# A hybrid trunk on one core: a second convolution chunk on VectorE, its taps spread among the S5 states, and TensorE's small products of the even mixer in blocks

## The chip, the cores and the metric

The kernel runs on one core of a Trainium2 chip. The core has five engines with instruction streams of their own: TensorE (PE in the profile; PEld are its weight loads), VectorE (DVE), ScalarE (ACT), GpSimd (POOL) and SyncE (SP), which here only issues transfers. Engines wait for each other by semaphores, and each works through its instructions in the order in which they were put on it. What counts is the device time of one execution in microseconds. The kernel before has a median of 1348.53 us over three runs (1348.24 to 1348.56).

## What is computed

One sequence of 512 positions with 1024 channels goes through two layers, each a mixer and a gated feed-forward block, with a norm ahead of each, residual adds, and a final norm. All values are float32. The even layer's mixer joins four retention heads with a Mamba-2 state-space part of 16 heads in chunks of 128 positions; the odd layer's joins a causal depthwise convolution over 31 positions with an S5 state-space part:

```python
def even_mixer(h, ...):
    ...
    r = head_group_norm(retention_chunkwise(q, k, v)).reshape(b, l, RET_V)
    y_ret = jax.nn.silu(g) * r
    ...
    y = ssd_chunked(xs, dt, a_neg, bm, cm)      # y_diag + y_off
    ...
def ssd_chunked(...):
    ...
    y_diag = jnp.einsum("bcijgh,bcjghp->bcighp", cb[..., None] * lmat, X)
    y_off = jnp.einsum("bcign,bcghpn->bcighp", Cc, prev) * jnp.exp(acs)[..., None]

def odd_mixer(h, ...):
    ca, cg, u = split_cols(h @ w_in, [512, 512, 512])
    c = ca * jax.nn.sigmoid(cg)
    c = causal_dwconv(c, conf_dw_w, conf_dw_b)                 # 31 taps, per channel
    c = jax.nn.silu(layer_norm(c, conf_ln_g, conf_ln_b))
    s = jax.nn.gelu(s5_ssm(u, ...))
    s = s * jax.nn.sigmoid(s @ s5_glu_w)
    return jnp.concatenate([c, s], axis=-1) @ w_out
```

## The kernel before

**Layout and stages.** Channels lie on the 128 partitions and the 512 positions along a row, so a tensor of 512 channels is four tiles of 128 x 512. The stages follow each other: even mixer, feed-forward, odd mixer, feed-forward, final norm. A projection (`proj`) splits weights and inputs into a high and a low part in a reduced float format and makes three matmuls for each 128 channels (`mm3`, L100 to L102). `wload` fetches the weights on SyncE's queue into `wraw` (four buffers), ScalarE casts the high part `whi` (L90), and VectorE subtracts to get the low part `wlo` (L91). `split` (L95, L96) does the same to inputs: `sh` on ScalarE and `slo` on VectorE for the S5 result, for instance. Matmuls that write `pyo`, `pyd`, `pcv`, `pS`, `pY` and the transposes are not of the split kind; they read float32 as it is.

**What sets the order.** The program is written in a certain order, and a scheduler with its own estimates of time lays the instructions out on each engine; `issue_after(x)` forbids it to put what follows ahead of `x`. Tiles come from rotating pools, so a load can wait until a buffer is free.

**Even mixer, `pair`.** Each of eight pairs of heads builds `ar` (decays times products, two tiles), `X` and the states `prev`. Then `pyo` gets three matmuls of 128 x 128 (L453; chunks 1 to 3, each from `prev` of the chunk before), and `pyd` eight of 64 x 128 (L458; four chunks of two heads). A matmul of this kind shows as two records in the profile. They stand on TensorE among the projections of whatever comes next (`pg`, `pxbc`, `po`), and the scheduler may put projections between them.

**Even mixer, `head`.** The normed result `yn` of each retention head is transposed in eight pieces (`pyT`, L564) to two tiles.

**Odd mixer.** `glu_in(i)` projects `ca` and `cg` of convolution chunk i. For a chunk in the list `PECONV` it writes the product twice to half-shifted tiles `cx` (VectorE, L848; the shifted halves copied by ScalarE, L850), and `conv_pe(i)` runs the 31 taps as 32 matmuls on TensorE (`pcv`, L891, 64 records), with weights `kd` that `conv_loads(i)` fetches in four transfers of 256 KB on SyncE's queue. Chunk 0 is not in the list: `conv(0, ...)` makes 30 multiply-adds on VectorE (L875), each on a whole tile with another shift, on top of a first tap by ScalarE. `s5_in(q)` projects `u`; `s5_state(q)` transposes it on TensorE (`pu2`, `puT`, with ScalarE's copies L916 and L922 between), makes the inputs of the states (`pS`, L930) and runs a chain of small VectorE operations (`s5rot`, L934 to L954) that ends in `sst`. `s5_y(q)` gives `pY` (L971, L974), ScalarE copies it out (L977), and `s5_split(q)` transposes it back (`pyT`, L984), applies the GELU (`sg`, L986) and splits it (`sh`, `slo`). "The S5 residue" in the title of the change is this low part `slo`. All four of them are inputs of the gate projection `pgl`.

The order as written before: chunks and states alternate; chunk 1's convolution stands ahead of `s5_state(3)`, chunk 2's between `s5_y(1)` and `s5_y(2)`, chunk 3's ahead of `s5_split(3)`; and the whole `conv(0)` on VectorE comes last, not before the state 3 chain is done.

**Start and end.** The packed constants `c1` (182 KB) are fetched on ScalarE's queue beside the first input tile, and the eight last output transfers are on SyncE's.

Of the kernel before, what the change touches and what calls it, by code (L numbers as in the profile page):

```python
# [15 lines left out]
P = 128  # L16
T = 512
NT = T // P
# [6 lines left out]
SH = 16  # L25
NPAIR = SH // 2
POOLTAPS = {}
PECONV = (1, 2, 3)
WV0 = (0, 1, 3, 6)
PACK0 = (("g_mix0", KC),)  # L30
PACK1 = (("ident", P), ("tri", P), ("cw", 48), ("cb", 12), ("dtb", SH), ("alog", SH), ("dsk", NPAIR),
         ("snw", NPAIR))
# [4 lines left out]
class Trunk:  # L37
# [197 lines left out]
    def finish(self, st, half, out):  # L235
        nc = self.nc
        ts = slice(half * T // 2, (half + 1) * T // 2)
        last = self.tmp("sq")[:, :T // 2]
        nc.scalar.activation(last, self.x[KC - 1][:, ts], AF.Square)
        self.gain(st, KC - 1, ts)  # L240
        if half == 0:
            st["p"] = self.ps("pstat")
            for t in range(NT):
                nc.tensor.matmul(st["p"][:, t:t + 1], lhsT=st["acc"][:, t * P:(t + 1) * P], rhs=self.onec, start=True,
                                 stop=True)
        p = st["p"][:, 2 * half:]
        for t in range(2):
            mark = nc.tensor.matmul(p[:, NT + t:NT + t + 1], lhsT=last[:, t * P:(t + 1) * P], rhs=self.onec, start=True,
                                    stop=True)
        v = self.small("fin_v", [P, 2])  # L250
        nc.vector.tensor_scalar(v, p[:, :2], 1.0 / D, EPS, op0=ALU.mult, op1=ALU.add)
        nc.vector.scalar_tensor_tensor(v, p[:, NT:NT + 2], 1.0 / D, v, op0=ALU.mult, op1=ALU.add)
        rs = self.rsqrt(v, [P, 2], "fin")
        for t in range(2):
            row = slice((2 * half + t) * P, (2 * half + t + 1) * P)
            for i in range(2):
                p = self.ps("pfin") if i else self.pp("pfin")
                with self.tc.issue_after(mark.ins):
                    for c in range(4):
                        nc.tensor.transpose(p[:, c * P:(c + 1) * P], self.x[4 * i + c][:, row], self.ident)  # L260
                o = self.slot("fin")
                if i == 0:
                    nc.scalar.activation(o, p, AF.Copy, scale=rs[:, t:t + 1])
                else:
                    nc.vector.tensor_scalar(o, p, rs[:, t:t + 1], None, op0=ALU.mult)
                nc.sync.dma_start(out[row, i * T:(i + 1) * T], o)

    def load_params(self):
        self.unpack("c2", PACK2, self.nc.gpsimd)
# [3 lines left out]
    def load_x(self):  # L273
        nc = self.nc
        st = self.norm_begin("mix0")
        st["w"] = []
        for c in range(KC):
            nc.sync.dma_start(self.x[c], self.ins["xT"][c])
            self.norm_chunk(st, c, False)
            if c in WV0:  # L280
                n = min([k for k in (*WV0, KC) if k > c]) - c
                hi, lo = self.wload(self.ins["wv0"][:, c * 272:(c + n) * 272], n * 272)
                st["w"] += [[w[:, k * 272:k * 272 + 272] for w in (hi, lo)] for k in range(n)]
            if c == 0:
                self.unpack("c1", PACK1, nc.scalar)
                self.ident = self.c["ident"]
        return st


    def even(self, st, prep):  # L290
        nc = self.nc
# [114 lines left out]
        def pair(pr, grp):  # L406
# [37 lines left out]
            for c in range(1, NT - 1):  # L444
                for h in range(2):
                    a0, a1 = (c - 1) * P + h * 64, c * P + h * 64
                    nc.vector.scalar_tensor_tensor(pv[:, a1:a1 + 64], pv[:, a0:a0 + 64],
                                                   cdl[:, c, 2 * pr + h:2 * pr + h + 1], p[:, a1:a1 + 64],
                                                   op0=ALU.mult, op1=ALU.add)
            po = self.ps("pyo")  # L450
            for c in range(1, NT):
                s = slice(c * P, (c + 1) * P)
                nc.tensor.matmul(po[:, s], lhsT=pv[:, (c - 1) * P:c * P], rhs=Ct[g][:, s], start=True, stop=True)  # L453
            pd = self.ps("pyd")
            for c in range(NT):
                for h in range(2):
                    s = slice(c * P, (c + 1) * P)
                    nc.tensor.matmul(pd[64 * h:64 * h + 64, s], lhsT=X[:, c * P + 64 * h:c * P + 64 * h + 64],  # L458
                                     rhs=ar[h][:, s], start=True, stop=True)
            y = self.slot("y")  # L460
            nc.vector.scalar_tensor_tensor(y, xc, dsk[:, pr:pr + 1], pd, op0=ALU.mult, op1=ALU.add)
            nc.vector.tensor_tensor(E[:, P:], E[:, P:], po[:, P:], op=ALU.mult)
# [52 lines left out]
        def head(h):  # L515
# [40 lines left out]
            for b in range(NT):  # L556
                s = slice(256 * (b % 2), 256 * (b % 2) + 256)
                nc.scalar.activation(yn[b // 2][:, s], py[b // 2][:, s], AF.Identity, scale=rs[:, b:b + 1],
                                     bias=nm[:, b:b + 1])
            for f in range(2):  # L560
                p = self.ps("pyT")
                for b in range(NT):
                    c0 = 256 * (b % 2) + f * P
                    nc.tensor.transpose(p[:, b * P:(b + 1) * P], yn[b // 2][:, c0:c0 + P], self.ident)  # L564
                nc.vector.tensor_tensor(gs[f], gs[f], p, op=ALU.mult)
                hi, lo = self.slot("mh", F32R), self.slot("ml", F32R)
                self.split(gs[f], hi, lo)
                mix[2 * h + f] = (hi, lo)
# [249 lines left out]
    def odd(self, st):  # L818
# [175 lines left out]
        def s5_loads(q):  # L994
            w1 = [self.slot("w1") for _ in range(2)]
            for ri in range(2):
                ld(w1[ri], self.w1d[ri, q])
            rot = self.slot("rot").rearrange("p (r x) -> p r x", r=2)
            ld(rot, self.rotd[0:2, q // 2, :, 256 * (q % 2):256 * (q % 2) + 256].rearrange("r p x -> p r x"))
            s5w[q] = (w1, rot)  # L1000
            if q % 2 == 0:
                rho = self.slot("rho")
                ld(rho, self.rotd[2, q // 2])
                s5rho[q // 2] = rho
# [13 lines left out]
            sx[q] = (hi, lo)  # L1018

        glu_in(0)  # L1020
        s5_loads(0)
        s5_loads(1)
        s5_in(0)
        glu_in(1)
        s5_state(0)
        s5_in(1)
        s5_loads(2)
        s5_loads(3)
        glu_in(2)
        s5_state(1)  # L1030
        s5_in(2)
        conv_loads(1)
        glu_in(3)
        s5_state(2)
        s5_in(3)
        conv_pe(1)
        states = s5_state(3)
        conv_loads(2)
        for q in range(4):
            out_loads(q)  # L1040
        y2[0] = s5_y(0)
        y2[1] = s5_y(1)
        s5_split(0)
        conv_pe(2)
        conv_loads(3)
        y2[2] = s5_y(2)
        s5_split(1)
        y2[3] = s5_y(3)
        s5_split(2)
        conv_pe(3)  # L1050
        s5_split(3)
        conv(0, after=states)
        mix = [None] * 8
        for m in range(4):
            p = self.pp("pgl")
# [166 lines left out]
```

## Time and profile before

| | us |
|---|---|
| median of three runs | 1348.53 |
| the profiled execution | 1349.29 |
| its span, first to last instruction | 1347.5 |
| one convolution on TensorE, 898.51 to 912.00 in the trace | 13.49 |
| sum of the 30 multiply-adds on VectorE (13.19 + 9.87 busy) | 23.06 |

Prices and places are read in the profiled execution, so sums are made against its 1349.29 us, which is the span and 1.8 us around it. A row of a timeline gives the start, the time from the first start to the last end, the engine, the line, the operation, the output and inputs with their shapes, how many like instructions follow each other, and in brackets the idle time of the engine ahead of it with what ended it. Matmuls overlap, so what one costs is the distance from its start to the next one's start.

### The profile page before, as it was taken

To read this page: it belongs to the slowest core of one execution; us is meant where nothing else is said; L and a number is where in the kernel's file an instruction comes from. 1 tells how busy PE (TensorE), PEld (TensorE's weight loads), DVE (VectorE), ACT (ScalarE), POOL (GpSimd) and SP (SyncE) were. 2 spreads that over 40 slices of the span, in tenths; PEclk is the share of its full clock that TensorE was granted. 3 is DMA by queue.
4 is the path that set the end of the run, shared out by engine and by line. 5 is a ranking of instruction groups with operands and counts; after the bars stand their busy time and mean duration, and the time that the engine had idled before them with its cause. 6 is when DMAs were issued, how large, how long until landed. Compare 5 with 4: busy or idle time off the path is not lost.

```text
span 1347.5 us, 17450 instructions
## 1 busy us (share of the span) xinstructions
PE 1333.4 (99%) x6676; PEld 1088.8 (81%) x6676; DVE 908.1 (67%) x1544; ACT 551.2 (41%) x775; POOL 160.9 (12%) x284
## 2 busy tenths in 40 slices
PE   9999999999999999999999999999999999999997
PEld 8778888888878888888888888557888888888887
DVE  6887877679688889787634346486877777773233
ACT  5454545454334444444423233235644444442221
POOL 0210010000570333860000000000000000000000
PEclk9999999999999999999999999999999999999999
DMA  6532234232264343543333344322433333333321
GB/s 226 158 114 83 71 93 120 70 104 85 79 175 127 116 125 112 151 135 104 90 92 100 98 129 161 125 95 63 134 96 105 97 94 94 96 99 89 100 71 63
DMA packets 50532, 146.16 MB, mean 108 GB/s; under 512 B 6544, under 2 KB 7872, under 8 KB 50448
## 3 DMA queue, kind: packets, MB, share of 16 engines
q1 hardware_dynamic: 44288, 127.49, 30.7%
q0 software_dynamic: 5872, 17.37, 4.5%
q8 instruction: 52, 0.85, 0.3%
q14 instruction: 32, 0.26, 0.1%
q10 hardware_dynamic: 288, 0.19, 0.0%
HBM read 135.03 MB, written 9.99 MB: 108 GB/s over the span
## 4 chain that ended last, share of the span: by engine, by line
PE 94%; DVE 3%; ACT 1%; issue 1%; DMA 0%; SPq 0%; DVEq 0%; ACTq 0%
PE pup L100 12%; PE pup L102 12%; PE pup L101 12%; PE pdn L101 6%; PE pdn L100 6%; PE pdn L102 6%; PE pcv L891 3%; PE po L102 3%; PE po L100 3%; PE po L101 3%; PE pxbc L101 1%; PE pxbc L100 1%; PE pxbc L102 1%; PE pqk L100 1%; PE pg L101 1%; PE pg L100 1%
## 5 line engine op out<-in xcount | busy, mean ns | idle before, releaser
L90 ACT CAST whi<-wraw 128x1024 fp32r<-128x1024 f32 (+3 forms) x246 | 231.2, 940 | 490.3 <-PE pup L101 140.9
L91 DVE TENSOR_TENSOR wlo<-wraw,whi 128x1024 fp32r<-128x1024 f32 (+3 forms) x246 | 269.8, 1098 | 140.7 <-ACT whi L90 140.7
L100 PE MATMUL pup<-xh,whi 128*128 128x512 f32 x704 | 274.7, 390 | 0.0
L102 PE MATMUL pup<-xh,wlo 128*128 128x512 f32 x704 | 274.0, 389 | 0.0
L101 PE MATMUL pup<-xl,whi 128*128 128x512 f32 x704 | 273.9, 389 | 0.0
L102 PEld LDWEIGHTS pup<-xh,wlo 128*128 128x128 f32 x704 | 132.2, 188 | 27.4
L101 PEld LDWEIGHTS pup<-xl,whi 128*128 128x128 f32 x704 | 132.2, 188 | 27.4
L100 PEld LDWEIGHTS pup<-xh,whi 128*128 128x128 f32 x704 | 132.2, 188 | 27.2
L100 PE MATMUL pdn<-acth,whi 128*128 128x512 f32 (+1 forms) x374 | 140.9, 377 | 0.0
L101 PE MATMUL pdn<-actl,whi 128*128 128x512 f32 (+1 forms) x374 | 140.8, 377 | 0.0
L102 PE MATMUL pdn<-acth,wlo 128*128 128x512 f32 (+1 forms) x374 | 140.8, 377 | 0.0
L190 DVE SCALAR_TENSOR_TENSOR ffa<-ffh,c,ffa 128x511 f32<-128x511 f32 (+1 forms) x176 | 134.6, 766 | 3.0
L185 DVE TENSOR_TENSOR ffh<-pup,R 128x512 f32<-128x512 f32 x88 | 60.5, 687 | 65.1 <-PE pup L102 64.9
L232 POOL TENSOR_SCALAR x<-x,c 128x512 f32<-128x512 f32 (+1 forms) x9 | 9.1, 1016 | 734.5 <-ACT acc L128 635.1
L187 ACT ACTIVATE ffa<-ffh,c 128x512 f32<-128x512 f32 x88 | 71.8, 816 | 40.0 <-DVE ffh L185 37.3
L100 PEld LDWEIGHTS pdn<-acth,whi 128*128 128x128 f32 x374 | 70.4, 188 | 13.0
L102 PEld LDWEIGHTS pdn<-acth,wlo 128*128 128x128 f32 x374 | 70.4, 188 | 12.9
L101 PEld LDWEIGHTS pdn<-actl,whi 128*128 128x128 f32 x374 | 70.4, 188 | 12.8
L102 PE MATMUL po<-mh,wlo 128*128 128x512 f32 x192 | 75.7, 394 | 0.6 <-DVE wlo L91 0.6
L100 PE MATMUL po<-mh,whi 128*128 128x512 f32 x192 | 75.4, 394 | 0.7 <-ACT mh L95 0.7
L101 PE MATMUL po<-ml,whi 128*128 128x512 f32 x192 | 75.6, 394 | 0.0
L95 ACT CAST acth<-ffg 128x512 fp32r<-128x512 f32 x44 | 27.3, 621 | 92.8 <-DVE ffg L197 88.2
(418 smaller groups left out, 2220.0 us busy)
## 6 DMA issues: line engine op xcount, KB each, us to landing
wraw<-in_wup_dram SPq DMA_DIRECT2D x88, 512.0 KB, 3.6
wraw<-in_wdn_dram SPq DMA_DIRECT2D x32, 512.0 KB, 3.6
wraw<-in_weo_dram SPq DMA_DIRECT2D x32, 256.0 KB, 3.1
wraw<-in_wxbc_dram SPq DMA_DIRECT2D x12, 512.0 KB, 3.8
wraw<-in_wdn_dram SPq DMA_DIRECT2D x16, 384.0 KB, 3.2
wraw<-in_wz_dram SPq DMA_DIRECT2D x8, 512.0 KB, 3.6
wraw<-in_wg_dram SPq DMA_DIRECT2D x8, 512.0 KB, 3.6
ar<-acd POOLq DMA_DIRECT2D x16, 256.0 KB, 3.8
```

What stands on the lines that cost most here:

```text
L90: nc.scalar.copy(hi[:, :n], raw[:, :n])
L91: (eng or nc.vector).tensor_tensor(lo[:, :n], raw[:, :n], hi[:, :n].bitcast(F32), op=ALU.subtract)
L95: self.nc.scalar.copy(hi, src)
L100: mm(out, lhsT=w[0], rhs=x[0], start=start, stop=False)
L101: mm(out, lhsT=w[0], rhs=x[1], start=False, stop=False)
L102: self.mark = mm(out, lhsT=w[1], rhs=x[0], start=False, stop=stop)
L185: nc.vector.tensor_tensor(h, p, st["R"], op=ALU.mult)
L187: nc.scalar.activation(a, h, AF.Identity, scale=dw[:, j, 2:3], bias=db[:, j:j + 1])
L190: nc.vector.scalar_tensor_tensor(a[:, s:], h[:, :T - s], dw[:, j, tap:tap + 1], a[:, s:], op0=ALU.mult, op1=ALU.add)
L232: self.nc.gpsimd.tensor_scalar(self.x[c][:, ts], self.x[c][:, ts], st["g"][:, c:c + 1], 1.0, op0=ALU.mult, op1=ALU.mult)
L891: self.mark = mm(p[64 * g:64 * g + 64, s:], lhsT=w, rhs=cin[i][g][:, :T - s], start=j == 0, stop=j == 15)
```

## The change

**A.** `PECONV` loses chunk 1, whose 30 taps go to VectorE too. The taps of chunks 0 and 1 are spread over the stage with fixed places: 1 to 8 of chunk 0 behind its product, 9 to 17 not before state 0's chain, 18 to 24 not before state 1's, 25 to 30 and taps 1 to 4 of chunk 1 not before state 2's; 5 to 12 of chunk 1 not before state 3's, and 13 to 30 not before the third `slo`. Chunk 2's convolution on TensorE moves ahead of state 3. **B.** In `pair`, the `pyo` matmuls run in the order 3, 1, 2 in a chain, and `pyd` behind them. **C.** In `head`, the four `pyT` pieces begin with the last, and the others follow it. **D.** `c1` is fetched on SyncE's queue behind the fifth input tile, and one of each two last output transfers goes to ScalarE's queue.

```diff
-PECONV = (1, 2, 3)
+PECONV = (2, 3)
...
-                nc.sync.dma_start(out[row, i * T:(i + 1) * T], o)
+                (nc.sync if i else nc.scalar).dma_start(out[row, i * T:(i + 1) * T], o)
...
-            if c == 0:
-                self.unpack("c1", PACK1, nc.scalar)
+            if c == 4:
+                self.unpack("c1", PACK1, nc.sync)
...
             po = self.ps("pyo")
-            for c in range(1, NT):
-                s = slice(c * P, (c + 1) * P)
-                nc.tensor.matmul(po[:, s], lhsT=pv[:, (c - 1) * P:c * P], rhs=Ct[g][:, s], start=True, stop=True)
+            off = None
+            for c in (3, 1, 2):
+                with self.tc.issue_after(off.ins) if off else nullcontext():
+                    s = slice(c * P, (c + 1) * P)
+                    off = nc.tensor.matmul(po[:, s], lhsT=pv[:, (c - 1) * P:c * P], rhs=Ct[g][:, s], start=True,
+                                           stop=True)
             pd = self.ps("pyd")
-            for c in range(NT):
-                for h in range(2):
+            with self.tc.issue_after(off.ins):
+                for c in range(NT):
+                    for h in range(2):
...
+            first = None
             for f in range(2):
                 p = self.ps("pyT")
-                for b in range(NT):
-                    c0 = 256 * (b % 2) + f * P
-                    nc.tensor.transpose(p[:, b * P:(b + 1) * P], yn[b // 2][:, c0:c0 + P], self.ident)
+                for b in (3, 0, 1, 2):
+                    with self.tc.issue_after(first.ins) if first else nullcontext():
+                        c0 = 256 * (b % 2) + f * P
+                        t = nc.tensor.transpose(p[:, b * P:(b + 1) * P], yn[b // 2][:, c0:c0 + P], self.ident)
+                    first = first or t
...
         glu_in(0)
+        conv(0, range(1, 9))
...
-        s5_state(0)
+        conv(0, range(9, 18), after=s5_state(0))
...
-        s5_state(1)
+        conv(0, range(18, 25), after=s5_state(1))
         s5_in(2)
-        conv_loads(1)
         glu_in(3)
-        s5_state(2)
+        states = s5_state(2)
+        conv(0, range(25, 31), after=states)
+        conv(1, range(1, 5), after=states)
         s5_in(3)
-        conv_pe(1)
+        for i in PECONV:
+            conv_loads(i)
+        conv_pe(2)
         states = s5_state(3)
-        conv_loads(2)
         for q in range(4):
             out_loads(q)
-        y2[0] = s5_y(0)
-        y2[1] = s5_y(1)
-        s5_split(0)
-        conv_pe(2)
-        conv_loads(3)
-        y2[2] = s5_y(2)
-        s5_split(1)
-        y2[3] = s5_y(3)
-        s5_split(2)
+        for q in range(4):
+            y2[q] = s5_y(q)
+            if q:
+                s5_split(q - 1)
         conv_pe(3)
         s5_split(3)
-        conv(0, after=states)
+        conv(1, range(5, 13), after=states)
+        conv(1, range(13, 31), after=ev[2])
```

The first place is TensorE's order at the first pair of the even mixer, before (`pyo` and `pyd` are the pair's two small products, `pg` a retention head's gate projection):

```order
L102 MATMUL pg<-xh,wlo 128x512
L453 MATMUL pyo<-CT,prev 128x128
L458 MATMUL pyd<-ar,X 64x128
L100 MATMUL pg<-xh,whi 128x512
L458 MATMUL pyd<-ar,X 64x128 x4
L453 MATMUL pyo<-CT,prev 128x128
L458 MATMUL pyd<-ar,X 64x128 x2
L453 MATMUL pyo<-CT,prev 128x128
L458 MATMUL pyd<-ar,X 64x128
L101 MATMUL pg<-xl,whi 128x512
```

And the same place of the change:

```order
L102 MATMUL pg<-xh,wlo 128x512
L100 MATMUL pg<-xh,whi 128x512
L456 MATMUL pyo<-CT,prev 128x128 x3
L463 MATMUL pyd<-ar,X 64x128 x8
L101 MATMUL pg<-xl,whi 128x512
L102 MATMUL pg<-xh,wlo 128x512
```

Seven pieces with a projection matmul between them have become two that follow each other; so it is at all eight pairs.

The second place is VectorE's order at the end of the S5 part, before: the last taps of chunk 0 (`cv_6995`), the residues (`slo`) and the first weight split of the gate projection.

```order
L875 SCALAR_TENSOR_TENSOR cv_6995<-ca,c_456,cv_6995 128x485
L875 SCALAR_TENSOR_TENSOR cv_6995<-ca,c_456,cv_6995 128x484
L875 SCALAR_TENSOR_TENSOR cv_6995<-ca,c_456,cv_6995 128x483
L875 SCALAR_TENSOR_TENSOR cv_6995<-ca,c_456,cv_6995 128x482
L96 TENSOR_TENSOR slo<-sg,sh 128x512 x3
L91 TENSOR_TENSOR wlo<-wraw,whi 128x512
```

In the change, behind the chain of state 3 (whose last row is the first here), the eight taps 5 to 12 of chunk 1 (`cv_7120`) and the first three residues:

```order
L962 TENSOR_TENSOR sst<-s5rot 64x4x63
L883 SCALAR_TENSOR_TENSOR cv_7120<-ca,c_456,cv_7120 128x507
L883 SCALAR_TENSOR_TENSOR cv_7120<-ca,c_456,cv_7120 128x506
L883 SCALAR_TENSOR_TENSOR cv_7120<-ca,c_456,cv_7120 128x505
L883 SCALAR_TENSOR_TENSOR cv_7120<-ca,c_456,cv_7120 128x504
L883 SCALAR_TENSOR_TENSOR cv_7120<-ca,c_456,cv_7120 128x503
L883 SCALAR_TENSOR_TENSOR cv_7120<-ca,c_456,cv_7120 128x502
L883 SCALAR_TENSOR_TENSOR cv_7120<-ca,c_456,cv_7120 128x501
L883 SCALAR_TENSOR_TENSOR cv_7120<-ca,c_456,cv_7120 128x500
L96 TENSOR_TENSOR slo<-sg,sh 128x512 x3
L883 SCALAR_TENSOR_TENSOR cv_7120<-ca,c_456,cv_7120 128x499
```

And some rows later in the change the end of the taps 13 to 30, with the fourth residue behind them:

```order
L883 SCALAR_TENSOR_TENSOR cv_7120<-ca,c_456,cv_7120 128x485
L883 SCALAR_TENSOR_TENSOR cv_7120<-ca,c_456,cv_7120 128x484
L883 SCALAR_TENSOR_TENSOR cv_7120<-ca,c_456,cv_7120 128x483
L883 SCALAR_TENSOR_TENSOR cv_7120<-ca,c_456,cv_7120 128x482
L96 TENSOR_TENSOR slo<-sg,sh 128x512
L91 TENSOR_TENSOR wlo<-wraw,whi 128x512
```

Before, the fourth residue stood behind the third with nothing between; now eighteen taps stand between them.

The third place is VectorE's order around chunk 2's gated product, before, from the end of state 0's chain to the clearing of the next state tile:

```order
L954 TENSOR_TENSOR sst<-s5rot 64x4x63
L840 TENSOR_TENSOR ca<-pca,R 128x512
L91 TENSOR_TENSOR wlo<-wraw,whi 128x1024 x2
L849 MEMSET cx 64x1
L841 TENSOR_TENSOR cg<-pcg,R 128x512
L91 TENSOR_TENSOR wlo<-wraw,whi 128x1024
L848 TENSOR_TENSOR cx<-ca,cg 64x512 x2
```

And in the change, with taps of chunk 0:

```order
L848 TENSOR_TENSOR ca<-pca,R 128x512
L883 SCALAR_TENSOR_TENSOR cv_6995<-ca,c_456,cv_6995 128x502
L91 TENSOR_TENSOR wlo<-wraw,whi 128x1024
L883 SCALAR_TENSOR_TENSOR cv_6995<-ca,c_456,cv_6995 128x501
L883 SCALAR_TENSOR_TENSOR cv_6995<-ca,c_456,cv_6995 128x500
L849 TENSOR_TENSOR cg<-pcg,R 128x512
L883 SCALAR_TENSOR_TENSOR cv_6995<-ca,c_456,cv_6995 128x499
L91 TENSOR_TENSOR wlo<-wraw,whi 128x1024
L883 SCALAR_TENSOR_TENSOR cv_6995<-ca,c_456,cv_6995 128x498
L856 TENSOR_TENSOR cx<-ca,cg 64x512
L883 SCALAR_TENSOR_TENSOR cv_6995<-ca,c_456,cv_6995 128x497
L856 TENSOR_TENSOR cx<-ca,cg 64x512
```

One more tap stands right ahead of these rows, so seven taps have come ahead of the last `cx`.

More of the change, by code (lines that the diff above doesn't have):

```diff
@@ L450, in pair @@
             po = self.ps("pyo")
-            for c in range(1, NT):
-                s = slice(c * P, (c + 1) * P)
-                nc.tensor.matmul(po[:, s], lhsT=pv[:, (c - 1) * P:c * P], rhs=Ct[g][:, s], start=True, stop=True)
-            pd = self.ps("pyd")
-            for c in range(NT):
-                for h in range(2):
-                    s = slice(c * P, (c + 1) * P)
-                    nc.tensor.matmul(pd[64 * h:64 * h + 64, s], lhsT=X[:, c * P + 64 * h:c * P + 64 * h + 64],
-                                     rhs=ar[h][:, s], start=True, stop=True)
+            off = None
[4 more added lines that the diff above has]
+                                           stop=True)
+            pd = self.ps("pyd")
+            with self.tc.issue_after(off.ins):
+                for c in range(NT):
+                    for h in range(2):
+                        s = slice(c * P, (c + 1) * P)
+                        nc.tensor.matmul(pd[64 * h:64 * h + 64, s], lhsT=X[:, c * P + 64 * h:c * P + 64 * h + 64],
+                                         rhs=ar[h][:, s], start=True, stop=True)
             y = self.slot("y")
```

## The prediction

> **What bounds the kernel now.** I began with the page: busy time by engine, then the chain that ended last.
>
> ```profile
> PE 1333.4 (99%) x6676; PEld 1088.8 (81%) x6676; DVE 908.1 (67%) x1544; ACT 551.2 (41%) x775; POOL 160.9 (12%) x284
> PE 94%; DVE 3%; ACT 1%; issue 1%; DMA 0%; SPq 0%; DVEq 0%; ACTq 0%
> ```
>
> TensorE works 99% of the span and is 94% of the chain, so time falls where TensorE gets less to do, as long as what it then waits for is on time. Those averages hide the one stage in which VectorE has room, the odd mixer; the busy time by stretches shows it (columns: window, length, busy of PE, PEld, DVE, ACT, POOL with counts, clock, DMA share, GB/s).
>
> ```profile
> 860.00:880.00 20.00, 18.74 (x178) 10.25 (x174) 8.22 (x21) 4.02 (x12) 0.00 (x0) 1.00 0.72 248
> 880.00:900.00 20.00, 20.00 (x155) 9.87 (x155) 19.17 (x30) 9.01 (x18) 0.00 (x0) 1.00 0.22 82
> ```
>
> VectorE is idle for 11.8 us of the first stretch (20 − 8.22) and full in the second, where the 30 taps of chunk 0 stand. TensorE's timeline there, with the last of its three convolutions (`pcv`):
>
> ```profile
> 873.48 0.72 PE L920 MATMUL puT<-c,u 64*128 64x64 f32 x8 [0.58 <-ACT u L916]
> 874.88 1.15 PE L930 MATMUL pS<-us,w 128*64 128x64 f32 x32 [0.68 <-ACT us L922]
> 875.87 0.39 PE L971 MATMUL pY<-toep,us 128*64 128x128 f32 x4
> ...
> 898.51 13.55 PE L891 MATMUL pcv<-cx,kd 128*64 128x512 f32 x64
> 912.00 0.71 PE L984 MATMUL pyT<-c,y 64*128 64x64 f32 x8
> ...
> 915.36 0.50 PE L101 MATMUL pgl<-slo,whi 128*128 128x512 f32 x1 [0.17 <-DVE slo L96]
> ```
>
> From one row's start to the next, a convolution takes 13.49 us (898.51 to 912.00), and TensorE meets only three short waits. The last one matters below: the eleventh `pgl` matmul waits for `slo` of the fourth S5 residue.
>
> **Part 1, one convolution leaves TensorE.** Removed: 64 records, 13.5 us, all on the path. Added: 30 taps on VectorE. Their price is in VectorE's timeline:
>
> ```profile
> 876.08 0.42 DVE L934 TENSOR_TENSOR s5rot<-pS,rot 128x256 f32<-128x256 f32 x1 [11.66 <-PE pS L930]
> ...
> 882.49 13.19 DVE L875 SCALAR_TENSOR_TENSOR cv<-ca,c,cv 128x511 f32<-128x511 f32 x17
> 895.60 0.68 DVE L96 TENSOR_TENSOR slo<-sg,sh 128x512 fp32r<-128x512 f32 x1
> 896.20 9.87 DVE L875 SCALAR_TENSOR_TENSOR cv<-ca,c,cv 128x494 f32<-128x494 f32 x13
> 905.99 1.29 DVE L96 TENSOR_TENSOR slo<-sg,sh 128x512 fp32r<-128x512 f32 x2
> 914.61 0.69 DVE L96 TENSOR_TENSOR slo<-sg,sh 128x512 fp32r<-128x512 f32 x1 [7.34 <-ACT sh L95]
> ```
>
> Seventeen taps take 882.49 to 895.60, 0.771 us each; thirteen take 0.753. Sixty taps are 45.7 us. Of them 34 go ahead of S5 state 3: 24 between the products and splits of chunks 1 to 3, ten into the 11.66 us in which VectorE waited. (That idle stays: a convolution, now chunk 2's, still stands ahead of state 3 on TensorE; ten taps are 7.7 us.) Eight stand behind the state's own chain, and eighteen between the third and the fourth `slo`.
>
> **The tail**, counted from the start of `pY` (t = 0; before: 875.87). VectorE: the state's chain ends at 6.6 (882.49), eight taps at 12.8. Then come three `slo` in one piece, which need ScalarE's third `sh`. TensorE would have `pY` 0 to 2 and the transposes done near 8.4, ScalarE copies out:
>
> ```profile
> 877.83 1.28 ACT L977 COPY y<-pY 64x256 f32<-64x256 f32 x4 [3.00 <-PE pY L974]
> ...
> 912.75 1.18 ACT L986 ACTIVATE sg<-pyT 128x512 f32<-128x512 f32 x1
> 913.96 0.62 ACT L95 CAST sh<-sg 128x512 fp32r<-128x512 f32 x1
> ```
>
> Four copies are 1.3 to 1.6 us, `sg` and `sh` 1.8 (912.75 to 914.58); by these rows and one table load the third `sh` comes at 13.8, so the three `slo` end near 14.6. The eighteen taps, at 0.753 to 0.771, take 13.7 and end at 28.3, the fourth `slo` at 29.0: the eleventh `pgl` starts there. Before, it started at 915.36 − 875.87 = 39.5. TensorE alone would be there at 26.3 (its four `pY` groups with a wait of 0.75 for the copies, one convolution of 13.5, the transposes and ten matmuls). So it waits some 2.7 us, and of the 13.5 us, 39.5 − 29.0 = 10.5 is left: **−13.5 + 3.0**. I take 3.0; it is 0 if the taps ran beside everything, and 4.5 if the third `sh` comes 1.5 later (a full group of copies).
>
> Here a rule of the Trainium skill speaks against the change. The rows first, after TensorE's last work (0.82 us from 1339.78):
>
> ```profile
> 1339.78 0.82 PE L260 MATMUL pfin<-c,x 128*128 128x128 f32 x6
> ```
> ```profile
> 1344.00:1345.00 1.00, 0.00 (x0) 0.00 (x0) 0.00 (x0) 0.00 (x0) 0.00 (x0) 0.82 1.04 387
> ```
>
> The work ended at 1340.6, and the granted clock (0.82 as the mean of this window) fell inside it. If it fell to one half, it did so 0.36 us before the window's end: 1344.6, 4.0 us after the last matmul. "TensorE: Matmul & The Clock Gate" of the Trainium skill (Part 1, What's actually happening) has the clock halved after an idle window of about 3.4 us, which the trace agrees with. By it a wait of 2.7 us keeps the clock, and one of 4 would slow the `pgl` behind it; that is rival F.
>
> **The front.** Ahead of state 3, taps now stand between VectorE's products, so `cx` and ScalarE's copies come later. Before, for chunk 2:
>
> ```profile
> 832.46 1.40 DVE L848 TENSOR_TENSOR cx<-ca,cg 64x512 f32<-64x512 f32 x2
> ```
>
> These two ended at 833.86. Now seven taps (5.4 us) stand ahead of the second, partly where VectorE idled; walked from the end of state 0's chain it ends at 835.8, and with it `u`, behind the copies of `cx` on ScalarE's queue, comes 2 us later. Projection matmuls hide part: by walking the new order I get waits at `puT` and `pS` of 0.2 (state 0), 0.95 (state 1) and 0.6 (state 2). Bounds: 0, and 3 x 1.26 = 3.8 if each state waited bare as state 3 does (0.58 + 0.68 above). **+1.8**. The loads of chunks 2 and 3 on SP's queue go ahead of the `toep` loads and behind `woo`; they land some 2.6 us before chunk 2's convolution needs them, by a landing time of 5.2:
>
> ```profile
> DMA to landing us min/median/max: 3.5/5.2/6.0
> ```
>
> **Part 2, blocks in the even mixer.** The eighth of the pairs:
>
> ```profile
> 302.87 0.39 PE L100 MATMUL po<-mh,whi 128*128 128x512 f32 x1
> 303.10 0.38 PE L453 MATMUL pyo<-CT,prev 128*128 128x128 f32 x2
> 303.41 0.43 PE L458 MATMUL pyd<-ar,X 128*64 128x128 f32 x2
> 303.77 0.50 PE L101 MATMUL po<-ml,whi 128*128 128x512 f32 x1
> 304.21 0.66 PE L458 MATMUL pyd<-ar,X 128*64 128x128 f32 x8
> 304.79 0.49 PE L453 MATMUL pyo<-CT,prev 128*128 128x128 f32 x2
> 305.21 0.65 PE L458 MATMUL pyd<-ar,X 128*64 128x128 f32 x6
> 305.79 0.50 PE L102 MATMUL po<-mh,wlo 128*128 128x512 f32 x1
> 306.13 0.38 PE L453 MATMUL pyo<-CT,prev 128*128 128x128 f32 x2
> 306.27 0.48 PE L100 MATMUL po<-mh,whi 128*128 128x512 f32 x1
> 306.59 0.39 PE L101 MATMUL po<-ml,whi 128*128 128x512 f32 x1
> ```
>
> A projection matmul takes 0.23 us here (302.87 to 303.10; 0.2275 over many). 302.87 to 306.59 is 3.72 with four of them, so `pyo` and `pyd` cost 2.81 net. The eight pairs, each measured so (the first from 61.91, this one the last): 3.31, 2.45, 2.44, 2.81, 3.15, 2.79, 3.15, 2.81, together 22.9. The changes of kind are dear: two `pyo` records ahead of `pyd` take 0.31, where the records themselves start 0.107 apart; a projection ahead of `pyd` 0.44, one after it 0.34. In one block: six `pyo` 0.31 + 4 x 0.107 = 0.74; sixteen `pyd`, growing 0.22 per four records from 0.58 for six or eight, 1.02; and 0.11 for the projection behind: 1.87, eight times 15.0. **−7.9**. Bounds: none of it if what a change of kind costs is set by something else, and 22.9 − 8 x 1.65 = 9.7 without any change inside. A block waits for its latest operand (`prev` or `ar`), where single pieces could start with the first. For `pyo` TensorE waited once before:
>
> ```profile
>   ACT prev L443: 0.3, 1
> ```
>
> The new order puts the blocks about where the last pieces stood, 7.7 us or more behind `pX`, so I take no wait; C prices one.
>
> **Small edits.** The `pyT` of the heads go from 19 pieces to 8 (full-array transposes between projections, nearly free in the trace): −0.2, between 0 and −1. `c1`:
>
> ```profile
> c<-in_c_dram ACTq DMA_DIRECT2D x1, 182.0 KB, 3.4
> ```
>
> 182 KB at the 387 GB/s of the window above are 0.47 us by which they delay `x` and the first weights; moved behind half of `x`, they give back at most that: −0.3, between 0 and −0.5. At the end one of two output transfers per block goes to another queue, but the window from 1344 shows the DMA engines full (1.04): 0, between −0.3 and 0.3.
>
> **Sum** on the profiled execution, 1349.29 (span 1347.5): −13.5 + 3.0 + 1.8 − 7.9 − 0.2 − 0.3 = −17.1, so 1332.2. The median of the runs is 0.76 lower; the same difference gives **1331.4**.
>
> **Rivals.**
> - B, VectorE hides nearly all: tail and front cost 0 to 1.5 instead of 4.8, so 1326.6 to 1328.1. For it: VectorE's waits of 11.66 and 7.34 us before. Against: eighteen taps stand ahead of the last `slo`, and they are 13.7 us.
> - C, blocks wait: `prev` and `ar` come 0.7 us late on each pair; 5.6 comes back: 1337. For it: `ar` needs a transfer, subtraction, `Exp` and product; against: 7.7 us of room.
> - D, slower than before, with VectorE as the bound: from the state's chain to the last `slo` stand 26 taps and three or four splits. It ends even with before when all gains (10.5 + 6.6 more from the other terms) are used up, so when that stretch takes 17.1 us more: 26 taps at 0.77 + 0.66 = 1.43 us. At 1.6 us (26 x 0.83 = 21.6) it would be 1353.0. Against: thirty taps at 0.75 to 0.77 in the same stage.
> - E, the blocks do nothing (a change of kind costs the same wherever it stands): 1331.4 + 7.9 = 1339.3. Against: x8 and x6 of `pyd` take the same 0.58, so the pieces cost, not the records.
> - F, the wait at `pgl` passes 4 us and the clock halves: 1.5 more of wait, and some fifteen `pgl` at 0.23 more each while it is half, 3.4: with both, 1336.5.
>
> **Chances.** Forecast within 2.5 us 0.52; B 0.15; C 0.13; F 0.06; E 0.09; D 0.03; 0.02 for a loss elsewhere that just eats the gain. 1326.5 to 1338.5 takes in the forecast, B, C and F, with the 10.5 to 13.5 of the tail and the bounds of the front. A measurement can tell about 0.2%, 2.7 us: faster 0.95, same 0.02, slower 0.03.
>
> **What would show it.** Of the changed kernel: no `pcv` of chunk 1; a wait of 2 to 3.5 us on TensorE at the eleventh `pgl`, put down to `slo` (under 1: B; clock below 1.00 behind it: F); waits at `puT` and `pS` of states 0 to 2 near 1.8 together; for each pair one piece of 6 `pyo` and 16 `pyd` records of about 1.9 us (over 2.5, or a wait for `prev` or `ar` ahead of it: C or E); taps at 0.75 to 0.77 (over 1: D). The forecast is wrong above all if the third `sh` comes much later than 13.8, since everything behind it on VectorE moves with it.

## The result, and the profile after

The change takes 1339.34 us (median of four runs, 1338.08 to 1340.04); the kernel before takes 1348.55 (four runs, 1348.24 to 1348.65). The ratio is 0.993 (0.9918 to 0.9943): 9.2 us faster, where 17.1 were forecast, and 0.8 us above the upper end of the range. The runs also lie farther apart, 2.0 us where those of before lie within 0.4. The profiled execution took 1340.04 (span 1338.3), 9.25 less than that of before.

Busy time by engine, as on the page of the change:

```profile
PE 1316.7 (98%) x6612; PEld 1084.1 (81%) x6612; DVE 928.4 (69%) x1571; ACT 550.1 (41%) x773; POOL 160.2 (12%) x284
```

TensorE's 6612 records are the 64 fewer of one convolution. Its timeline at the end of the odd mixer's S5 part, as for before:

```profile
873.51 0.73 PE L928 MATMUL puT<-c,u 64*128 64x64 f32 x8 [0.56 <-ACT u L924]
874.91 1.15 PE L938 MATMUL pS<-us,w 128*64 128x64 f32 x32 [0.68 <-ACT us L930]
875.90 0.39 PE L979 MATMUL pY<-toep,us 128*64 128x128 f32 x4
...
885.22 0.71 PE L992 MATMUL pyT<-c,y 64*128 64x64 f32 x8 [0.58 <-ACT y L985]
...
904.97 0.50 PE L101 MATMUL pgl<-slo,whi 128*128 128x512 f32 x1 [1.96 <-DVE slo L96]
```

The last row is the matmul that reads the fourth residue. It is the eleventh `pgl` in the order of before and is called so below; here two `pgl` matmuls of the next part have come ahead of it, so it is the thirteenth. From the first `pY` to it are 29.07 us (904.97 − 875.90); 29.0 were forecast, and 39.5 it was before. VectorE's rows say why:

```profile
890.59 13.73 DVE L883 SCALAR_TENSOR_TENSOR cv<-ca,c,cv 128x499 f32<-128x499 f32 x18
904.23 0.68 DVE L96 TENSOR_TENSOR slo<-sg,sh 128x512 fp32r<-128x512 f32 x1
```

The eighteen taps took 13.64 us up to the start of the residue (13.7 forecast), and the residue starts 28.3 us behind `pY`, as forecast. But `pY` starts where it started before (875.87), although the even mixer ahead of it should have become some 8 us shorter, with only 1.8 of that lost again in the front. So most of the loss lies further forward. TensorE's waits there over 0.7 us, of which before showed none:

```profile
157.62 0.50 PE L100 MATMUL pg<-xh,whi 128*128 128x512 f32 x1 [2.16 <-DVE kT L498]
...
379.23 0.50 PE L102 MATMUL po<-mh,wlo 128*128 128x512 f32 x1 [2.75 <-DVE wlo L91]
```

and the windows of 2 us of the change ahead of its last matmul in which the granted clock is not 1.00 (it stands behind the five engines' busy times, ahead of the DMA share and the GB/s):

```profile
158.00:160.00 2.00, 2.00 (x8) 1.62 (x7) 2.00 (x5) 1.08 (x2) 0.00 (x0) 0.74 0.46 180
160.00:162.00 2.00, 2.00 (x6) 1.52 (x5) 1.70 (x2) 0.00 (x0) 0.00 (x0) 0.50 0.00 0
162.00:164.00 2.00, 2.00 (x8) 1.52 (x8) 0.00 (x0) 0.00 (x0) 0.00 (x0) 0.91 0.39 131
...
906.00:908.00 2.00, 2.00 (x7) 1.60 (x6) 0.69 (x1) 1.97 (x3) 0.00 (x0) 0.62 0.11 12
908.00:910.00 2.00, 2.00 (x6) 1.52 (x6) 1.21 (x2) 1.21 (x4) 0.00 (x0) 0.53 0.35 127
```

Behind the wait for `kT`, and behind that of the eleventh `pgl`, TensorE ran at half clock for a while. Each time (0.26 + 0.50 + 0.09) x 2 = 1.70 us of clock are lost, and (0.38 + 0.47) x 2 = 1.70, so 3.4 us at one half. Before had nothing of the kind ahead of its last matmul.

The blocks are as forecast. The eighth pair in the change:

```profile
302.37 0.39 PE L100 MATMUL po<-mh,whi 128*128 128x512 f32 x1
302.60 0.83 PE L456 MATMUL pyo<-CT,prev 128*128 128x128 f32 x6
303.35 1.09 PE L463 MATMUL pyd<-ar,X 128*64 128x128 f32 x16
304.38 0.50 PE L101 MATMUL po<-ml,whi 128*128 128x512 f32 x1
304.71 0.39 PE L102 MATMUL po<-mh,wlo 128*128 128x512 f32 x1
```

302.37 to 304.71, less two projections, is 1.88 us, where 1.87 were forecast and 2.81 stood before. No `pyo` or `pyd` waits for an operand.

So the theory (W in the expectations): every part costs what was forecast, and the rest was lost to two waits that the new order in the even mixer brought, neither of them for the blocks' own operands, and to a clock that halves behind such waits, the forecast wait at `pgl` among them. The rivals were that the blocks or the conv part hurt themselves, and that the clock fell for other reasons.

### The profile page after: what moved, and what is told of

The parts are those of the page before. It is cut to its first block, busy times and chain, and to the rows that moved or that the text cites. A ratio compares the mean times of both kernels' runs of the same rounds, so it can differ in the third digit from the quotient of the medians.

```text
span 1338.3 us, 17351 instructions
## 1 busy us (share of the span) xinstructions
PE 1316.7 (98%) x6612; PEld 1084.1 (81%) x6612; DVE 928.4 (69%) x1571; ACT 550.1 (41%) x773; POOL 160.2 (12%) x284
## 3 DMA queue, kind: packets, MB, share of 16 engines
q10 hardware_dynamic: 720, 1.05, 0.2%
```

## The experiments

All times are medians; the kernel before had 1348.6 to 1348.8 beside them. Four kernels first: the parts B and A alone, and an attempt at two of the waits.

**e1: part B alone.** The kernel before with the diff's lines of `pair`, nothing else.

> The kernel before with part B alone (pyo and pyd in blocks). Theory W (the blocks cost what was forecast, 15.1 us instead of 22.9, and the loss is in waits that the new order of the even mixer brings: about 2.2 us for kT and 1.6 of half clock behind it, 2.1 more for a weight split at the S5 products): 1348.5 - 7.8 + 5.9 = about 1346.6, with the wait for kT near 157 us and granted clock below 1.00 behind it. Rival R (the waits of the changed kernel come from the other parts, or the blocks hurt themselves by waiting for prev and ar): 1340.7 without these waits, or waits of pyo or pyd on prev or ar.

1345.80 us (1343.87 to 1347.59, seven runs), ratio 0.9974 (0.9963 to 0.9985). Its timeline of TensorE has the wait for `kT` without the other parts,

```profile
157.73 0.50 PE L100 MATMUL pg<-xh,whi 128*128 128x512 f32 x1 [2.16 <-DVE kT L497]
```

and its windows of 2 us the half clock behind it:

```profile
158.00:160.00 2.00, 2.00 (x7) 1.54 (x7) 2.00 (x5) 1.18 (x2) 0.00 (x0) 0.59 0.53 211
160.00:162.00 2.00, 2.00 (x7) 1.59 (x6) 1.81 (x3) 0.00 (x0) 0.00 (x0) 0.56 0.00 0
```

The wait for the weight split at the S5 products, which W had put down to the blocks too, is not there (0.59 us at 388, as before); without it W's sum is 1344.5. The seven runs fall in two groups, three at 1343.9 to 1344.2 with a mean granted clock of 0.998, four at 1345.8 to 1347.6 with 0.996 or 0.997.

**e2: part A alone.** The kernel before with `PECONV = (2, 3)` and the new order of the odd mixer.

> The kernel before with part A alone (second chunk on VectorE, taps spread). Theory W: -13.5 + 1.6 (front) + 2.9 (wait at the eleventh pgl and its like) + 1.5 (clock at one half behind that wait) = -7.5, so about 1341.0, and windows with a clock near 0.5 some 1 to 5 us behind the wait. Rival G (the clock does not depend on that wait): -9.0, 1339.5, clock 1.00 there.

1340.70 (1340.23 to 1341.02), ratio 0.9938 (0.9921 to 0.9954). The eleventh `pgl` waits 1.96 us, and the clock falls behind it:

```profile
906.00:908.00 2.00, 2.00 (x7) 1.58 (x7) 0.69 (x1) 1.66 (x2) 0.00 (x0) 0.67 0.00 0
908.00:910.00 2.00, 2.00 (x6) 1.52 (x6) 0.69 (x1) 0.84 (x2) 0.00 (x0) 0.50 0.51 133
910.00:912.00 2.00, 2.00 (x10) 1.66 (x9) 1.20 (x2) 1.62 (x3) 0.00 (x0) 0.97 0.02 6
```

W holds, G falls. Two of the four runs have a mean clock of 0.999, the profiled one 0.998, and they are only 0.6 and 0.8 us faster, so these runs do not show the full price of the half clock. The gain of 8.0 us is 13.5 less front, tail and clock.

**e3: five taps behind the fourth residue.**

```diff
-        conv(1, range(13, 31), after=ev[2])
+        conv(1, range(13, 26), after=ev[2])
+        conv(1, range(26, 31), after=ev[3])
```

> The changed kernel with taps 26 to 30 of chunk 1 behind the fourth residue (13 to 25 stay ahead of it). Theory W: the wait of 1.96 us at the eleventh pgl goes and the half clock behind it too: 1339.3 - 3.5 = about 1335.8, clock 1.00 from 895 to 925. Rival G (clock falls for another reason): -2.0, about 1337.3. Rival V (VectorE's next splits become late instead): no gain, 1339, with waits of pgl or po on wlo or mh.

1337.63 (1336.87 to 1338.53), ratio 0.9916 (0.9902 to 0.9931). In the trace the wait is 0.15 us and the clock there 1.00, no wait came instead, but only 1.7 of the 3.5 us arrived. The profile shows why in this execution: now the clock fell behind the other wait, where it had stayed at 1.00 in the profile of the change. The wait in the timeline of e3:

```profile
379.76 0.50 PE L102 MATMUL po<-mh,wlo 128*128 128x512 f32 x1 [2.75 <-DVE wlo L91]
```

and the windows of e3 behind it:

```profile
380.00:382.00 2.00, 2.00 (x7) 1.57 (x7) 2.00 (x3) 0.19 (x1) 2.00 (x2) 0.71 0.34 116
382.00:384.00 2.00, 2.00 (x6) 1.57 (x5) 2.00 (x2) 1.67 (x3) 2.00 (x3) 0.50 0.15 38
384.00:386.00 2.00, 2.00 (x9) 1.60 (x9) 2.00 (x3) 0.00 (x0) 1.98 (x3) 0.94 0.65 191
```

The same wait, the same 2.75 us, once with and once without the half clock. What tells the two apart is worked out at the end of the section on why the prediction was wrong.

**e4: ScalarE's copies first.** What stands right ahead of `kT` is ScalarE's queue; its timeline in the change:

```profile
154.06 1.05 ACT L90 CAST whi<-wraw 128x1024 fp32r<-128x1024 f32 x1 [7.03 <-PE pv L514]
155.01 0.63 ACT L131 ACTIVATE sq<-y 128x512 f32<-128x512 f32 x1
155.66 0.58 ACT L496 COPY rot<-pqk 64x512 f32<-64x512 f32 x1
```

A cast for `pg` waits 7 us for its buffer, and the pair's `sq` and the copies of the rotated keys are queued behind it. The edit keeps the cast behind the copies (`rot_mark` is the last of the copies `rot`, noted where it is issued):

```diff
-                self.proj(p, ins["wg"][2 * h + f], xs)
+                with self.tc.issue_after(self.rot_mark.ins):
+                    self.proj(p, ins["wg"][2 * h + f], xs)
```

> The changed kernel, but the gate projection of a retention head (its weight casts among it) is not put ahead of the copies of the rotated q and k on ScalarE. Theory W: the wait of pg for kT (2.16 us at 157.6) and the half clock behind it go: 1339.3 - 3.8 = about 1335.5. Rival: the wait moves to the next consumer (the casts of the scores, or the gate weights), no gain, about 1339.

1347.37 (1346.53 to 1352.29), ratio 0.9993: a miss. The edit applies to all heads, and at the first one TensorE now waits 6.28 us for the cast that was held back, with the clock at 0.50 from 66 to 72. TensorE's timeline in e4:

```profile
68.95 0.80 PE L100 MATMUL pg<-xh,whi 128*128 128x512 f32 x1 [6.28 <-ACT whi L90]
```

The rival was right: the wait went to the gate weights.

**e5: without part C.** The change with `pyT` written as before.

> The changed kernel without part C (the pyT of the retention heads in the order of before). Theory W: C itself gives nothing, but it shifted one weight split of VectorE behind the S5 products; that wait (2.75 us at 379) goes back to the 0.6 of before, and with it the half clock that sometimes follows: 1339.3 - 2.1 to 3.5 = 1336 to 1337. Rival P (contiguous transposes are a gain as forecast, and the wait comes with the blocks): 1339.5, wait still there.

1335.97 (1334.72 to 1336.41), ratio 0.9903 (0.9886 to 0.9919), 3.4 us faster than the change. The wait of 2.75 us at 379 is gone, and at 388.15 stands one of 0.62 us, which the change had lost and which before had too:

```profile
391.82 0.50 PE L102 MATMUL po<-mh,wlo 128*128 128x512 f32 x1 [0.62 <-DVE wlo L91]
```

So it was part C that brought the long wait. VectorE's timeline in the change shows how: the split stands behind one product more than before.

```profile
371.24 0.95 DVE L782 TENSOR_TENSOR w2r<-s5p,s5m 128x512 f32<-128x512 f32 x1
372.11 1.10 DVE L783 TENSOR_TENSOR s5u<-s5p,s5m 128x512 f32<-128x512 f32 x1
373.14 1.80 DVE L785 TENSOR_TENSOR w2i<-s5p,s5m 128x512 f32<-128x512 f32 x1
374.86 1.12 DVE L784 TENSOR_TENSOR w2r<-w2r,s5u 128x512 f32<-128x512 f32 x1
375.91 0.67 DVE L581 TENSOR_TENSOR x<-x,po 128x512 f32<-128x512 f32 x1
376.51 1.21 DVE L786 TENSOR_TENSOR s5u<-s5p,s5m 128x512 f32<-128x512 f32 x1
377.64 1.54 DVE L91 TENSOR_TENSOR wlo<-wraw,whi 128x512 fp32r<-128x512 f32 x1
```

These are 6.4 us of products and an addition from 371.24 to 377.64, none of which TensorE needs now, ahead of the split that it does need. Before, a split stood right ahead of the first product and another between them:

```profile
372.21 0.80 DVE L91 TENSOR_TENSOR wlo<-wraw,whi 128x512 fp32r<-128x512 f32 x1
...
378.08 1.10 DVE L91 TENSOR_TENSOR wlo<-wraw,whi 128x512 fp32r<-128x512 f32 x1
```

**e6: the fourth pair as before.** The order of `pyo` and `pyd` is left free for pair number 3 alone.

```diff
-            for c in (3, 1, 2):
-                with self.tc.issue_after(off.ins) if off else nullcontext():
+            for c in (3, 1, 2) if pr != 3 else (1, 2, 3):
+                with self.tc.issue_after(off.ins) if off and pr != 3 else nullcontext():
...
-            with self.tc.issue_after(off.ins):
+            with self.tc.issue_after(off.ins) if pr != 3 else nullcontext():
```

> The changed kernel with the products of the fourth pair (number 3) free in order as before, the other seven in blocks. Theory W: pyo and pyd of that pair cost 0.9 more, but stand 13 matmuls of pv earlier on TensorE; the wait for kT (2.16) and the half clock behind it (1.6) go: 1339.3 - 2.9 = about 1336.4. Rival K (kT is late because of ScalarE's queue, whatever the order of the pair): wait stays, about 1340.

1336.28 (1336.16 to 1337.70), ratio 0.991 (0.9896 to 0.9925), 3.1 us faster than the change. `pg` starts with no wait, and the clock stays 1.00 from 158 to 164:

```profile
157.03 0.50 PE L100 MATMUL pg<-xh,whi 128*128 128x512 f32 x1
```

The pair's products cost 0.9 us more and the loss of 3.9 is gone; K falls. Two things differ in the traces. Counted from ScalarE's copy of `prev` (146.79 in the change, 147.14 in e6), the pair's products begin 3.38 us behind it in the change and 1.82 in e6, which is 13 `pv` matmuls at 0.12 us; TensorE has these matmuls left to cover the way to `kT`. And on ScalarE `sq` and the copies stand ahead of the cast, as before. There `sq` itself waits 7.04 us, for `y`, so what the cast costs in the change is about its own 1.05 us and not the 7 of its wait. How much each of the two gives was not taken apart.

**e7: all three.** No part C, the fourth pair free, five taps behind the fourth residue.

> The changed kernel with all three: the fourth pair free, pyT as before, taps 26 to 30 of chunk 1 behind the fourth residue. Theory W: the three losses add up (2.9 + 2.1 + 3.3): 1339.3 - 8.3 = about 1331.0, the clock 1.00 throughout, and a spread of the runs as small as that of the kernel before. Rival (the losses overlap, or new waits come): 1334 to 1336.

1332.37 (1331.97 to 1332.57), ratio 0.9879 (0.9864 to 0.9893): 7.0 us faster than the change and 16.3 faster than before. Its runs lie within 0.6 us, and its profile has no wait over 0.75 us ahead of the final norm and no half clock ahead of the last matmul. The single gains (1.7, 3.4 and 3.1) come to 1.2 us more than that; the half clock strikes some runs only, and may in part be counted in more than one of them.

**e8: part D alone.**

> The kernel before with part D alone (c1 on SyncE's queue behind the fifth input tile, one of each two last outputs on ScalarE's queue). Forecast: -0.3 (0 to -0.5) at the start, 0 at the end: 1348.4. Rival: -0.8 as the traces of before and of the change stand to each other at the first projections; then 1347.9. Theory S: nothing, since kernels with and without D show the same early start; 1348.7.

1348.89 (1348.30 to 1349.22, ten runs), ratio 1.0001 (0.9991 to 1.0010): nothing. The profile of before starts `pacs` at 41.50, the change at 40.72; but e2, which has no part D, starts it at 40.73. The profiled execution of before had begun late by 0.8 us, which also is by what it lies above the median.

**e9 to e12: how long a wait.** The clean kernel e7, with the taps placed so that the wait at the eleventh `pgl` grows. The edits change the bounds of the two ranges of taps; e11 and e12 also hold the fourth residue behind the last tap, and e12 keeps the four parts of `pgl` in order.

> The kernel of e7 with one tap instead of five behind the fourth residue: 17 taps ahead of it, so the eleventh pgl waits about 1.2 us (1.96 - 0.75). Theory N (the clock halves for 3.4 us, 1.7 us lost, where TensorE idles for more than about half of a 3.4 us window, and the windows run on their own): never here, 1332.4 + 1.05 = 1333.4, small spread. Rival L (as the prediction had it, about 4 us of idleness are needed): the same here. Rival A (any wait at this place brings it): 1335.1.

> The kernel of e7 with no tap behind the fourth residue: 18 ahead of it, wait 1.96 us. Theory N: two groups of runs, 1334.2 without and 1335.9 with the half clock, told apart by the mean granted clock (0.001 lower); spread about 2 us. Rival L: 1334.2 only, small spread. Rival A: 1335.9 only.

> The kernel of e7 with 20 taps between the third and the fourth residue and none behind it: wait about 3.5 us. Theory N: the half clock in nearly every run, 1332.4 + 3.3 + 1.7 = 1337.4, small spread. Rival L: 1335.7, clock 1.00. Rival A: 1337.4 too.

> The kernel of e11, but the matmuls of each part of the gate projection stay behind those of the part before, so that TensorE has nothing else to run: the eleventh pgl then waits about 3.8 us, 4.1 later than in e7. Theory N: the half clock in every run (no 3.4 us window with 3.8 us of idleness across it stays over half busy, at most two share it), 1332.4 + 4.1 + 1.7 = 1338.2, small spread, clock 0.5 for 3.4 us in the profile. Rival L (more than about 4 us of idleness are needed): 1336.5 and clock 1.00.

The wait in TensorE's timeline, for e9:

```profile
899.93 0.50 PE L101 MATMUL pgl<-slo,whi 128*128 128x512 f32 x1 [1.68 <-DVE slo L96]
```

for e10:

```profile
900.37 0.50 PE L101 MATMUL pgl<-slo,whi 128*128 128x512 f32 x1 [1.95 <-DVE slo L96]
```

for e11:

```profile
902.18 0.50 PE L101 MATMUL pgl<-slo,whi 128*128 128x512 f32 x1 [1.89 <-DVE slo L96]
```

and for e12:

```profile
902.20 0.50 PE L101 MATMUL pgl<-slo,whi 128*128 128x512 f32 x1 [3.96 <-DVE slo L96]
```

with the windows of e12, where (0.20 + 0.50 + 0.15) x 2 = 1.70 us of clock are lost (first three rows), and of e10, where the clock stays at 1.00 (last two):

```profile
902.00:904.00 2.00, 1.80 (x6) 1.51 (x7) 0.76 (x2) 1.25 (x2) 0.00 (x0) 0.80 0.00 0
904.00:906.00 2.00, 2.00 (x6) 1.51 (x6) 0.77 (x2) 1.25 (x2) 0.00 (x0) 0.50 0.45 90
906.00:908.00 2.00, 2.00 (x9) 1.60 (x8) 0.27 (x1) 0.92 (x2) 0.00 (x0) 0.85 0.13 49
...
900.00:902.00 2.00, 1.64 (x7) 1.37 (x8) 0.76 (x2) 1.08 (x2) 0.00 (x0) 1.00 0.04 8
902.00:904.00 2.00, 2.00 (x11) 1.65 (x10) 0.78 (x2) 1.99 (x4) 0.00 (x0) 1.00 0.24 85
```

| | wait in the profile | median | the runs |
|---|---|---|---|
| e9 | 1.68 | 1333.59 | 1333.24 to 1333.73, one group |
| e10 | 1.95 | 1334.47 | 1333.74, 1333.97 and 1334.97 (clock 0.999 in all three), 1335.48 (0.998) |
| e11 | 1.89 | 1334.89 | 1334.06, 1334.38 (clock 0.999) and 1335.40, 1335.55 (0.997) |
| e12 | 3.96 | 1337.89 | 1337.20 to 1338.62 (0.996 to 0.998) |

The sizes in e9 and e11 missed: the scheduler placed the other `pgl` matmuls differently (the waiting one is the eleventh in e9 and e12, the thirteenth in e10 and the twentieth in e11), so that e9 waits longer than meant and e11 is a second e10. Yet they tell the theories apart. At 1.68 us no run shows the half clock; at 1.9 the mean clock says that some runs of one kernel do and others don't, 1.2 us apart (e11), the profiles of e10 and e11 being of the faster kind; at 3.96 the profile shows it. The groups of e10 are less clear, since one of its two slower runs has the clock of the faster ones. Without it e12 would take 1336.2 (e7's 1332.37, and 3.96 less the 0.16 that e7 waits there); its median lies 1.7 above that, and all five runs lie above it. Rival L falls, since half clock followed waits of 1.96 and 2.16 us; rival A falls, since the profile of e10 has the clock at 1.00 behind 1.95 us.

## Why the prediction was wrong

**What bounds the kernel**: right. The chain of TensorE set the time, and everything that was lost was lost as its waits or its clock.

**The convolution and the tail**: right. The gain from `pY` to the eleventh `pgl` is 10.42 us (39.49 − 29.07), forecast 10.5. The third `sh` ended 14.1 us behind `pY` (forecast 13.8). The wait was 1.96 where 2.7 were expected, since two `pgl` matmuls (0.46) had come ahead of it, and the 0.58 of the transposes stood beside it where 0.75 were expected.

**The front**: right. From the first `pca` to `pY` it became 1.62 us longer in the traces, forecast 1.8; the waits of states 0 to 2, forecast as 0.2, 0.95 and 0.6, were none over 0.3, 0.70 and 0.59.

**The blocks**: right in their own price; the sum over all eight, worked out in the traces as in the prediction, is 15.15 us after 22.91, −7.76 against −7.9. The small edits: C gave nothing by itself in TensorE's time (at three of the four heads, where only projections stand between the `pyT`, they cost 3.87 us before and 3.94 in the change, net of the projections), and D nothing (e8), where −0.5 together were expected. The heads' `pyT` went from 15 pieces to 4; the prediction's 19 and 8 count in the four of the S5 part.

**The step that failed** is the one behind the blocks: "A block waits for its latest operand ... so I take no wait". It looked only at what the block waits for. What the moved block, and the moved transposes, do to the others on their queues was not priced, and it costs, in the trace of the change, 2.16 us (`kT`, by B: e1, e6), 2.13 (`wlo`, 2.75 instead of 0.62, by C: e5) and 1.70 of clock behind the first. That is 6.0 of the 7.85 us by which the profiled executions missed the sum. Taking C out and leaving pair 3 free, with the taps as in the change, gives back 4.9 us, measured (e10, 1334.47), although the pair itself then costs 0.9 more. Moving the five taps gives 2.1 more (e7), but 1.8 of that is the wait at `pgl`, which the forecast had in its sum.

**The second step that failed** is the clock: "By it a wait of 2.7 us keeps the clock". That 4.0 us of idleness were needed was read from a single place, the end of the kernel, where nothing follows that could show an earlier fall. "TensorE: Matmul & The Clock Gate" of the Trainium skill (Part 1, What's actually happening) asks for an idle window of about 3.4 us and lets the windows run on their own. The 3.4 us for which the clock stayed at one half agree with that length (six profiles, 1.70 us each). That waits of 1.96 and 2.16 us, not entirely idle windows, bring it doesn't agree, and the measurement decides. Behind the eleventh `pgl` it cost 1.19 us of the tail: from there to the last wait for `mh` of the odd mixer it took 36.46 after 35.27, though with two `pgl` matmuls fewer, so 1.65 like for like. Rival F had the mechanism with a chance of 0.06, asked for a wait over 4 us, and priced the half clock at 3.4 us, twice the 1.70 measured (its terms make 1336.3, not 1336.5).

The rivals: B, D and E fell. E's 1339.3 is the time that was measured, and that is chance: by E the blocks do nothing, and they gave 7.76 us. C had a near price, 5.6 us for blocks that wait, but another place: none of them waited. The late start of 0.78 us in the profile of before, which D did not cause, partly hid the loss in the sum of the profiled executions; some 0.9 us of the even mixer stay spread over small differences that no experiment took apart.

**When the clock falls.** By the length of the wait alone it looks arbitrary: in the profiles the clock fell behind all four waits for `kT` (2.16 us), behind two of seven at `pgl` of 1.9 to 2.0, and behind one of four at `wlo` (2.75). The traces hold more. The two half-clock pieces of the change begin at 158.97 and 906.49, and those of e3 at 158.97 and 380.84; both distances, 747.52 and 221.87, are whole multiples (219 and 65) of one step of 3.413 us, the length of a piece. Cut every profile into such steps from where its clock changes, and count in each step the time without a matmul (an estimate, since the ends of matmuls are modelled). In all 14 profiles the half clock followed every step with 1.90 us or more of it, and none with 1.81 or less. The longer wait escaped by where it lay: a step ends at 377.42, and of the change's wait for `wlo`, 376.48 to 379.23, 1.81 us fall into the next one; in e3 it lies at 377.01 to 379.76, 2.34 us fall into that step, and the clock halves behind it. The wait of e10 is cut into 1.55 and 0.40, that of the change at `pgl` leaves 1.90 in one step, and that of e12 is cut into 1.55 and 2.42. The 4.0 us at the end of the kernel before, from which the prediction took its limit, are the 0.6 us that were left of one step and a whole one.

**What stays open**: the share of a step that decides lies between 1.81 and 1.90 of 3.413 us as far as these traces go. No run set the place of the steps; the profiles mostly show them elsewhere in each execution, which fits the runs of one kernel that meet the half clock and those that don't, but that was not tried.

## What to carry to other kernels

Where a scheduler lays the order out, fixing a few instructions moves others: compare the new order with the old on the queues of all engines that feed the bound engine, above all for a split or cast that now stands behind work nobody waits for. A wait of the bound engine can cost more than itself: here one of 1.9 us or more could bring another 1.7 of half clock, when enough of it fell into one step of 3.4 us, so giving the engine other work in a long wait can be worth more than the wait's length (splitting a wait was not tried). A spread among runs of one kernel that before was not there, with the mean granted clock going with the time as in e1 and e11, points to that.

## What the runs showed of the hardware

- The half clock comes in pieces of the same size, 1.70 us lost in each of the change's two, and of those of e1, e3 and e12, and there its beginning lies 0.6 to 1.5 us behind the end of the wait, not in it: the wait of the change ended at 157.62, and the clock is at one half from 158.97, where a step of 3.413 us ends.
- The same product of two 128 x 512 tiles on VectorE took between 0.68 and 1.80 us. Two of its lines in the change, by shape (the three numbers are the shortest, the median and the longest, in ns):

```profile
L782 DVE TENSOR_TENSOR w2r<-s5p,s5m x4: 947/1778/1786, 371.2 to 511.1; 128x512 f32<-128x512 f32 x4
L785 DVE TENSOR_TENSOR w2i<-s5p,s5m x4: 678/680/1804, 373.1 to 516.0; 128x512 f32<-128x512 f32 x4
```

GpSimd's timeline in the change shows what lay beside the last of each, at 511.1 (long) and at 516.0 (short):

```profile
510.57 1.75 POOL L719 TENSOR_TENSOR w1r<-w1r,s5t 128x512 f32<-128x512 f32 x1
...
513.86 1.62 POOL L722 TENSOR_TENSOR w1i<-w1i,s5t 128x512 f32<-128x512 f32 x1
516.33 1.33 POOL L794 DMA_DIRECT2D w2d<-w2r  x2 [0.85 <-DVE w2r L784]
```

The long one has a product of GpSimd beside it, the short one a pause and the issue of DMAs. The 1.80 us of e5's fence, at 373.14, lie in a stretch in which GpSimd computes too, and the addition among those rows, one of whose inputs (`po`) TensorE wrote, took 0.67 beside the same work. "GPSIMD Engine Reference" of the Trainium skill (Specifications) says that GpSimd shares its way to SBUF with VectorE, and names instructions of VectorE with two inputs from SBUF among those that contend for it. These rows agree; that this is the cause was not tried. The long ones stand in the queue ahead of the split for which TensorE waits.
